# A two-layer diffusion block in float32: layer 0's gate and up products as Strassen's seven, its gated blocks through DRAM, and modulation pieces moved

## The chip, the cores and the metric

The kernel runs on one core of a Trainium2 chip. The metric is the device time of one execution in microseconds (us). The engines are TensorE (PE), VectorE (DVE), ScalarE (ACT), GpSimd (POOL) and SyncE (SP), which here only issues DMAs.

## The reference

Two layers over 512 latent and 256 context tokens of width 1024, all in float32. Each layer has modulated norms around an attention of three head groups, and around a gated feed-forward with hidden width 2816. What the change touches is the feed-forward and the modulation:

```python
def _swiglu(h, w_gate, w_up, w_down):
    return (jax.nn.silu(h @ w_gate) * (h @ w_up)) @ w_down
...
for l in range(DEPTH):
    last = l == DEPTH - 1
    mod = (silu_c @ w_ada[l] + b_ada[l])[:, None, :]
    mod_c = (silu_cc @ w_ada[l] + b_ada[l])[None, None, :]
    sh_a, sc_a, gt_a, sh_f, sc_f, gt_f = jnp.split(mod, 6, axis=-1)
...
    hf = _rms(x, g_ffn_pre[l]) * (1.0 + sc_f) + sh_f
    x = x + gt_f * _rms(_swiglu(hf, w_ffn_gate[l], w_ffn_up[l], w_ffn_down[l]), g_ffn_post[l])
    if not last:
        hfc = _rms(xc, g_ffn_pre[l]) * (1.0 + csc_f) + csh_f
        xc = xc + cgt_f * _rms(_swiglu(hfc, ...), g_ffn_post[l])
```

Layer 0 runs all 768 tokens through the feed-forward, layer 1 only the 512 latent ones.

## The kernel before, in words

**Precision.** A float32 product is made of three fast ones (`mm3`, L415): each operand is split into a rounded part and a residual (`copy`, L397, and `low`, L412, which computes x minus its rounded part). A weight tile is 128x1024 (four blocks of 128 rows by 256 columns, or two by 512): `weights` (L452) loads it (`st`), lets ACT write the rounded part `wh` and DVE or POOL the residual `wl`. Four of each are in a ring (`RING`).

**Order of the work.** Each stage collects steps in a `Plan` (L136), each with a rank, the engines that could do it with a cost for each, the steps it follows and the buffers it takes. `run` orders the steps by rank and by these costs and writes the program; the order on each engine is fixed from then on. The ranks come from a table of numbers at the head of the file.

**The stages**, the same in both layers: input projection (110 to 240 us in layer 0, 1137 to 1240 in layer 1), attention, out-projection (450 to 530; 1430 to 1475), gate and up (530 to 922; 1475 to 1713), down projection (922 to 1137; 1713 to the end). The out-projection takes the tokens in two passes; each token then gets its residual and norm (L703, L649), is modulated on DVE and POOL, transposed on PE (L663) and split into `hT`, the moving operand of gate and up. The chunk that follows runs in the same plan.

**Gate and up.** The hidden columns go in 11 chunks of 256. Chunk 0 (L1700) is plain in both layers. In layer 0 chunks 1 to 10 are plain too (L1890): per 128 hidden columns, 96 weight blocks are each multiplied with 512 latent and with 256 context tokens. ACT then takes silu of the gate, DVE multiplies it with up (L1899) into `a`, which stays in SBUF. In layer 1 chunks 1 to 10 (`by_sums`, L1749) are Strassen's product of a 2x2 split: the first two operands halve the tokens and the 1024 inputs, the other two are gate and up. Seven products of half size (L1813) take differences of weight tiles (`minus`, L1768, DVE or POOL) with sums of halves of `hT` (`sums_of_halves`, L1584), and their results are added up by DVE out of PSUM (L1841) and by DVE or POOL in SBUF (L1842, L1851 to L1862).

**Down.** `spread` (L1728) splits a block of `a` into the operand `sp`; `projected` multiplies it with the weights in two passes over the tokens of layer 0.

**Modulation.** `ada` (L486) makes one piece of 512 columns of `mod`: eight weight tiles of 256 KB are loaded, and DVE multiplies each with one scalar per partition and adds it to a sum (first L509, then seven times L511, a "mac"). A piece with two strands does so for `c` and for `c_ctx`; with one only for `c`. Each strand is split like an operand (L413) and summed over partitions by two matmuls of 512 columns (L527). Layer 0's gate and up holds 14 pieces with 20 strands; layer 0's input projection holds five pieces.

```python
for s, a in enumerate(acc):
    def mac(_, s=s, a=a, k=k, st=st):
        c = sc[:, s, k:k + 1]
        if k == 0:
            V.tensor_scalar(out=a.tile[:, :512], in0=st.tile[:, :512], scalar1=c, ...)
        else:
            V.scalar_tensor_tensor(out=a.tile[:, :512], in0=st.tile[:, :512], scalar=c,
                                   in1=a.tile[:, :512], op0=ALU.mult, op1=ALU.add)
```

## Time and profile before

| | us |
|---|---|
| median of 3 runs | 1841.51 (1840.59 to 1846.79) |
| the profiled execution | 1841.75 |
| its span in the trace | 1839.9 |
| PE busy | 1740.1 (95%) |
| DVE, ACT, POOL busy | 1245.7, 869.1, 880.3 |
| layer 0, gate and up from the first matmul to the last | 529.6 to 921.7 |
| layer 0, down projection | 922 to 1137 |
| layer 1, input projection | 1137 to 1240 |
| layer 1, gate and up | 1475.2 to 1713 |

The span is what the trace covers; the 1.85 us that the execution's own time has more lie around it. PE is busy nearly all the time, so its busy share alone says where it is slowed only where it falls; matmuls overlap in the records, and the time that one adds is the distance between two starts, not the length of a record. DVE and POOL records include time in which an operation stands still, so their means are compared with the same operation elsewhere.

### The profile page before, as it was taken

Reading aid. Unit: us, or ns where it says so; the run is one execution under the profiler, and the core shown is the slowest. Engines: PE = TensorE matmul, PEld = TensorE weight load, DVE = VectorE, ACT = ScalarE, POOL = GpSimd, SP = SyncE. Lnnn points to the kernel's source line nnn. Section 1 sums busy time; section 2 is a strip of 40 time slices with the busy share of each in tenths; the row PEclk is TensorE's granted clock in tenths of the full one; section 3 lists DMA queues with packets and bytes.
Section 4 is the critical chain, followed back from the end, with each engine's and each line's share of the span. In section 5 each row is a group of like instructions: output and inputs, shape, how many; then the busy total and the mean of one; then the engine's idle time right before and its main releaser. Section 6 shows DMA issues by size and latency. Waiting matters only on the chain. (4 is left out here: it accounts for less than half of the span.)

```text
span 1839.9 us, 28101 instructions
## 1 busy us (share of the span) xinstructions
PE 1740.1 (95%) x10290; PEld 1502.0 (82%) x10290; DVE 1245.7 (68%) x1728; ACT 869.1 (47%) x1792; POOL 880.3 (48%) x935
## 2 busy tenths in 40 slices
PE   6888799999999999999999898999999989999998
PEld 2676588788789888888888787978788789999886
DVE  6859878887575987521244745248989699998434
ACT  3344278997561221111233434538888545555212
POOL 3566967787362121000012628696878366543100
PEclk9889999999999999999999999999999999999999
DMA  9155103002644677321253432312101643331432
GB/s 309 58 151 161 51 22 84 13 2 71 212 142 123 209 223 252 124 71 46 82 182 126 137 126 91 93 53 53 44 2 62 202 161 116 126 103 59 160 95 77
DMA packets 135210, 205.79 MB, mean 112 GB/s; under 512 B 12920, under 2 KB 68696, under 8 KB 135072
## 3 DMA queue, kind: packets, MB, share of 16 engines
q1 hardware_dynamic: 135072, 203.99, 35.2%
q8 instruction: 81, 1.33, 0.3%
q14 instruction: 57, 0.47, 0.1%
HBM read 184.21 MB, written 9.52 MB: 105 GB/s over the span
## 5 line engine op out<-in xcount | busy, mean ns | idle before, releaser
L472 ACT CAST wh<-st 128x1024 fp32r<-128x1024 f32 (+2 forms) x177 | 183.5, 1039 | 337.5 <-PE m L419 141.4
L413 DVE TENSOR_TENSOR wl<-st,wh 128x1024 fp32r<-128x1024 f32 (+1 forms) x152 | 213.1, 1403 | 191.3 <-ACT wh L472 189.1
L1890 PE MATMUL m<-hT,wh 128*128 128x512 f32 (+1 forms) x1280 | 278.2, 339 | 0.0
L1890 PEld LDWEIGHTS m<-hT,wh 128*128 128x128 f32 x1280 | 196.6, 188 | 30.7 <-issue 0.8
L1385 ACT ACTIVATE P<-s,nm 128x768 f32<-128x768 f32 (+1 forms) x200 | 164.4, 826 | 25.8 <-DVE nm L1378 19.8
L417 PE MATMUL m<-wh,sp 128*128 128x512 f32 x440 | 171.9, 391 | 0.0
L418 PE MATMUL m<-wl,sp 128*128 128x512 f32 x440 | 171.5, 390 | 0.0
L419 PE MATMUL m<-wh,sp 128*128 128x512 f32 x440 | 171.3, 389 | 0.0
L1378 DVE TENSOR_REDUCE nm<-s 128x1 f32<-128x768 f32 x160 | 151.1, 950 | 23.5 <-PE s L1372 19.8
L1890 PE MATMUL m<-hT,wl 128*128 128x512 f32 (+1 forms) x640 | 164.7, 338 | 0.0
L511 DVE SCALAR_TENSOR_TENSOR acc<-st,sc,acc 128x512 f32<-128x512 f32 x182 | 141.8, 820 | 17.0 <-DMA st<-in_w_ada 15.9
L1813 PE MATMUL m<-hT,wh 128*128 128x256 f32 x800 | 145.0, 283 | 0.0
L418 PE MATMUL m<-wl,hT 128*128 128x512 f32 (+2 forms) x368 | 141.1, 383 | 3.0 <-DVE wl L413 1.8
L417 PE MATMUL m<-wh,hT 128*128 128x512 f32 (+2 forms) x368 | 143.3, 389 | 0.1
L419 PE MATMUL m<-wh,hT 128*128 128x512 f32 (+2 forms) x368 | 140.8, 383 | 2.6 <-POOL hT L413 2.6
L1813 PEld LDWEIGHTS m<-hT,wh 128*128 128x128 f32 x800 | 124.8, 192 | 0.0
L1813 PE MATMUL m<-hT,wl 128*128 128x256 f32 x400 | 113.4, 283 | 3.3 <-DVE wl L413 3.3
L1890 PEld LDWEIGHTS m<-hT,wl 128*128 128x128 f32 x640 | 98.7, 189 | 15.3
L413 DVE TENSOR_TENSOR wl<-x,wh 128x1024 fp32r<-128x1024 f32 x67 | 100.3, 1500 | 6.6 <-ACT wh L1773 6.5
L399 POOL TENSOR_SCALAR sp<-a 128x384 fp32r<-128x384 f32 (+1 forms) x11 | 9.0, 819 | 196.3 <-PE m L419 190.6
L1773 ACT CAST wh<-x 128x1024 fp32r<-128x1024 f32 x67 | 70.0, 1051 | 68.5 <-PE m L1813 33.5
L413 POOL TENSOR_TENSOR PT<-P,PT 128x384 fp32r<-128x384 f32 x93 | 95.6, 1033 | 3.7
(347 smaller groups left out, 4210.2 us busy)
## 6 DMA issues: line engine op xcount, KB each, us to landing
st<-in_w_ada SPq DMA_DIRECT2D x152, 256.0 KB
st<-in_w_ffn_down SPq DMA_DIRECT2D x66, 512.0 KB
...
```

The source lines that it names most:

```text
L399: G.tensor_scalar(out=out, in0=in_, scalar1=1.0, scalar2=0.0, op0=ALU.mult, op1=ALU.add)
L413: by(e).tensor_tensor(out=out, in0=src, in1=h.bitcast(F32), op=ALU.subtract)
L417: mm(ps, lhsT=a[0], rhs=b[0], start=start, stop=False)
L418: mm(ps, lhsT=a[0], rhs=b[1], start=False, stop=False)
L419: mm(ps, lhsT=a[1], rhs=b[0], start=False, stop=stop)
L472: a = plan.add(rank, {"act": c_act(W) + 0.05}, lambda _: A.copy(out=part(0)[:, :W], in_=st.tile[:, :W]), [x], kept[:1], [st])
L511: V.scalar_tensor_tensor(out=a.tile[:, :512], in0=st.tile[:, :512], scalar=c, in1=a.tile[:, :512], op0=ALU.mult, op1=ALU.add)
L1378: V.tensor_reduce(out=nm[:, 0:1], in_=S.tile[:, :768], axis=AX.X, op=ALU.max, negate=True)
L1385: A.activation(out=P.tile[:, c], in_=S.tile[:, c], func=AF.Exp, bias=box["nm"][:, i:i + 1], scale=1.0, accum_out=r_()[:, t + i:t + i + 1])
L1773: a = plan.add(rw, {"act": c_act(1024) + 0.05}, lambda _: A.copy(out=kept[0].tile, in_=x.tile), after, kept[:1], [x])
L1813: mm(m.tile[:, :n], lhsT=ww, rhs=moving[y](q, k), start=bool(first) and k == 0 and t == 0, stop=k == 3 and t == 2, skip_group_check=not first)
L1890: mm(o, lhsT=w, rhs=y[:, a:b, z, :], start=(k == 0 and i == 0), stop=(k == NK - 1 and i == 2))
```

## The change

Layer 0's gate and up become seven products in all 11 chunks. The tokens are put in the order of the two passes ([4, 5, 0] and [1, 2, 3]), which are the two halves of 384 tokens; so products have 384 columns, 168 of them a chunk. Layer 1's chunk 0 becomes seven products too, with 256 columns. Those products of chunks 0 to 2 which need only pass 1's tokens (1 and 2, 144 matmuls) are put ahead of the rest, beside pass 2's norms. In layer 0 the gated blocks are stored to DRAM by SP (`a_d`, 44 stores of 128x384) and read back in the down projection; and there the differences of weights and the sums and products in SBUF are POOL's alone (`only`, from chunk 1's second half on; chunks 0 and 1 begin on both). Of the 14 pieces of modulation in that stage four stay (6 strands); six go to layer 0's down projection (10 strands), four to layer 1's input projection (4 strands), where `P` has four buffers in place of seven.

```diff
-S_RANK = 26
+S_RANK = 5
-W_LATER = ((2, 512), (3, 0), (3, 512), (4, 0), (4, 512))
+W_LATER = (((2, 512), (3, 0), (3, 512), (4, 0), (4, 512)), ((3, 0), (3, 512), (4, 0), (4, 512)))
+F_LATER = ((0, 5, 0), (0, 5, 512), (1, 5, 0), (1, 5, 512))
+D_LATER = ((1, 0), (1, 512), (0, 0), (0, 512), (2, 0), (2, 512))
+D_ADA = (9, 12, 15, 18, 32, 38)
-F_ADA_STEP = 0.85
+F_ADA_STEP = 4.5
...
-            nw = W_PAIRS if l == 0 else 0
+            nw = W_PAIRS
...
+        if last:
+            aT = [fs.tile([128, TQ], F32, name=f"a{j}") for j in range(2)]
+        else:
+            a_d = [drp.tile([128, TQ], F32, name=f"ad{j}") for j in range(NH)]
...
+        parts7 = {1: ("a", "A11", 1), 5: ("c", "S1", 1), 7: ("d", "S3", 1), 6: ("b", "S2", 1), 2: ("a", "A12", 0),
+                  3: ("c", "S4", 0), 4: ("d", "A22", 0)}
...
+            def first(self, plan, rank, after=(), ways=("pool", "dve")):
+                l1, l2, self.l3 = (self.load(plan, rank, *q, after) for q in ((0, 0), (1, 0), (1, 1)))
+                x1, x2, x3 = self.xs[0, 0], self.xs[1, 0], self.xs[1, 1]
+                if self.whole:
+                    O[1] = self.split(plan, rank, x1, [l1])
+                t1 = self.minus(plan, rank, x1, x2, x1, [l1, l2, ...], ways)
+                O[5] = self.split(plan, rank, x1, [t1])
+                self.t3 = self.minus(plan, rank, x2, x3, x2, [self.l3, t1], ways)
+                O[7] = self.split(plan, rank, x2, [self.t3])
...
+                v = vec(both, plus(s7, s5, s7), [c.copied["c", jj], c.copied["d", jj]], (), [s5, s7])
+                u = vec({"dve": c_vec(n)}, psum_add(w, w, mb), [c.done[6, jj], c.copied["a", jj]], (), [w, mb])
+                y = vec({"dve": c_vec(n)}, psum_add(s5, w, mc), [c.done[3, jj], u, v], (), [w, s5, mc])
+                z = vec(both, plus(s7, w, s7), [u, v], (), [w, s7])
...
+                y = vec(both, lambda e, s5=s5, g1=g1: times(s5.tile, s5, g1)(e), [y, g], (), [s5, g1])
+                x = vec(both, lambda e, s7=s7, w=w: times(s7.tile, s7, w)(e), [z, x], (), [s7, w])
+                c.out += [(i, j, t, d) for i, (t, d) in enumerate(((s5, y), (s7, x)))]
+        def stored(plan, ch, rank):
+            for i, j, t, d in cs[ch].out:
+                plan.add(rank, {"sp": c_dma(n)}, lambda _, t=t, i=i, j=j: dma(
+                    out=a_d[j][:, i * n:(i + 1) * n], in_=t.tile), [d], (), [t], lag=2.2, writes=[("a", j, i)])
...
+            for ch in range(3):
+                columns_of(plan, ch, 20 + ch, 20 + ch, (1, 2), {i: w_f(plan, O_W0[l] + ch, ch, 0, u)
+                                                                for u, i in enumerate((1, 2))})
+            sums_of_halves(plan, full, S_RANK, taken)
+            ops[0].first(plan, O_W1[l], lds)
+            columns_of(plan, 0, 30, 30, (5, 7, 6, 3, 4), ops[0].second(plan, O_W1[l], lds))
+            ops[1].first(plan, O_W1[l] + 2, lds)
...
+                    after = [plan.add(rank - 1, {"sp": c_dma(w)}, lambda _: dma(out=rd.tile, in_=a_d[k][:, c0:c0 + w]), (),
+                                      [rd], lag=2.2, reads=[("a", k, pi)])]
...
+                for i, (al, v, c0) in enumerate(F_LATER):
+                    ada(plan, F_ADA[l] + F_ADA_STEP * i, al, v, c0, 2 - al, tiles, late=True)
+            only = ("pool", "dve") if last else ("pool",)
+            for ch in range(1, NH // 2):
+                if ch > 1:
+                    ops[ch].first(plan, rw, (), only)
+                columns_of(plan, ch, 2 * ch, 2 * ch + 1, (5, 7, 6, 3, 4) if ch <= 2 else (1, 5, 7, 6, 2, 3, 4),
+                           ops[ch].second(plan, rw, (), only), only)
+                if not last:
+                    stored(plan, ch, 2 * ch + 1)
...
+                for rk, (v, c0) in zip(D_ADA, D_LATER):
+                    ada(plan, rk, l + 1, v, c0, 2 if v < 2 else 1, tiles, late=True)
```

The change makes the lines of common functions three to five higher: `low` is L416, `copy` L402 or L404, the macs L512 and L514, the differences L1657, the products L1713, sums out of PSUM L1737, products and sums in SBUF L1740 and L1743, the stores L1767.

POOL, in a chunk of layer 0's gate and up past the first four, as the change orders it (`X`, `x` are weight tiles, `n` results of products): four differences and eight operations on results, which is a chunk's share.

```order
L1743 TENSOR_TENSOR n_4582<-n_4580,n_4582 128x384
L1743 TENSOR_TENSOR n_4590<-n_4588,n_4590 128x384
L1743 TENSOR_TENSOR n_4582<-n_4585,n_4582 128x384
L1743 TENSOR_TENSOR n_4590<-n_4589,n_4590 128x384
L1657 TENSOR_TENSOR X_4578<-X_4575,X_4578 128x1024
L1657 TENSOR_TENSOR X_4575<-x,X_4575 128x1024
L1657 TENSOR_TENSOR X_4578<-x,X_4578 128x1024
L1740 TENSOR_TENSOR n_4580<-n_4580,n_4583 128x384
L1740 TENSOR_TENSOR n_4588<-n_4588,n_4593 128x384
L1740 TENSOR_TENSOR n_4582<-n_4582,n_4585 128x384
L1740 TENSOR_TENSOR n_4590<-n_4590,n_4589 128x384
L1657 TENSOR_TENSOR x<-x,X_4578 128x1024
```

None of these stood there before: POOL had in layer 0's gate and up 25 instructions, for modulation pieces and the next stage.

DVE, in the third and fourth chunk of that stage, as the change orders it (`nf` are parts of a modulation piece, `m` is PSUM):

```order
L514 SCALAR_TENSOR_TENSOR nf<-nf,sc 128x512
L416 TENSOR_TENSOR wl<-X_4578,wh 128x1024
L1737 TENSOR_TENSOR n_4580<-n_4587,m_4600 128x384
L1737 TENSOR_TENSOR n_4582<-n_4588,m_4598 128x384
L514 SCALAR_TENSOR_TENSOR nf<-nf,sc 128x512 x2
L416 TENSOR_TENSOR wl<-X_4575,wh 128x1024
L1737 TENSOR_TENSOR n_4587<-n_4587,m_4599 128x384
L514 SCALAR_TENSOR_TENSOR nf<-nf,sc 128x512
L1737 TENSOR_TENSOR n_4588<-n_4588,m_4604 128x384
L514 SCALAR_TENSOR_TENSOR nf<-nf,sc 128x512
L416 TENSOR_TENSOR wl<-X_4578,wh 128x1024
L514 SCALAR_TENSOR_TENSOR nf<-nf,sc 128x512 x3
```

The residuals now come from tiles that POOL has made by subtraction, with macs between them; from the fifth chunk on the macs end.

DVE in the first pass of layer 0's down projection, before:

```order
L413 TENSOR_TENSOR wl<-st,wh 128x1024 x2
L413 TENSOR_TENSOR sp<-a_5640,sp 128x384
L413 TENSOR_TENSOR wl<-st,wh 128x1024 x2
L413 TENSOR_TENSOR sp<-a_5642,sp 128x384
L413 TENSOR_TENSOR wl<-st,wh 128x1024 x2
L413 TENSOR_TENSOR sp<-an,sp 128x384
```

and now:

```order
L416 TENSOR_TENSOR nr<-nf,nr 128x384
L416 TENSOR_TENSOR wl<-st,wh 128x1024
L514 SCALAR_TENSOR_TENSOR acc_8238<-st_8273,sc,acc_8238 128x512
L514 SCALAR_TENSOR_TENSOR acc_8241<-st_8273,sc,acc_8241 128x512
L416 TENSOR_TENSOR wl<-st,wh 128x1024
L514 SCALAR_TENSOR_TENSOR acc_8238<-st_8289,sc,acc_8238 128x512
L514 SCALAR_TENSOR_TENSOR acc_8241<-st_8289,sc,acc_8241 128x512
L514 SCALAR_TENSOR_TENSOR acc_8238<-st_8296,sc,acc_8238 128x512
L514 SCALAR_TENSOR_TENSOR acc_8241<-st_8296,sc,acc_8241 128x512
L514 SCALAR_TENSOR_TENSOR acc_8238<-st_8329,sc,acc_8238 128x512
L514 SCALAR_TENSOR_TENSOR acc_8241<-st_8329,sc,acc_8241 128x512
L416 TENSOR_TENSOR nr<-nf,nr 128x384 x2
```

The pieces' macs stand between the residuals of weights and of operands (`nr` is the operand, split from a block that was read back), and half of the residuals of weights went to POOL.

## Rows read from the trace of the kernel before

**Rows 1.** The page, part 1: busy time, share of the span, instructions

```profile
PE 1740.1 (95%) x10290; PEld 1502.0 (82%) x10290; DVE 1245.7 (68%) x1728; ACT 869.1 (47%) x1792; POOL 880.3 (48%) x935
```

**Rows 2.** Windows by stage: length, busy time (instructions) of each engine, clock, DMA

```profile
110.00:240.00 130.00, 107.40 (x480) 85.30 (x479) 106.20 (x170) 53.41 (x144) 102.23 (x104) 0.93 0.37 111
570.00:922.00 352.00, 348.64 (x1965) 298.75 (x1965) 196.74 (x272) 67.59 (x97) 34.86 (x25) 1.00 0.46 145
1137.00:1240.00 103.00, 100.54 (x503) 87.45 (x502) 34.20 (x65) 42.30 (x117) 86.38 (x116) 1.00 0.24 72
1504.00:1560.00 56.00, 51.06 (x406) 50.46 (x407) 52.69 (x55) 27.39 (x45) 32.03 (x22) 0.97 0.53 170
1560.00:1713.00 153.00, 153.00 (x1276) 152.96 (x1275) 138.96 (x148) 77.09 (x115) 70.83 (x63) 1.00 0.31 94
...
922.00:1020.00 98.00, 96.88 (x432) 79.76 (x431) 48.30 (x49) 38.83 (x59) 27.23 (x31) 1.00 0.46 149
```

**Rows 3.** PE's waits, 110 to 240 us, then 570 to 922: us, times, longest

```profile
PE m L527 <- ACT pair L401: 8.5, 2, 4.3
PE m L527 <- POOL pair L413: 5.5, 4, 2.5
...
PE m L527 <- DVE pair L413: 2.4, 2, 1.8
```

**Rows 4.** Line 1890 on PE: count, duration min/median/max, first and last start

```profile
L1890 PE MATMUL m<-hT,wh x1280: 277/337/500, 569.8 to 921.3; 128*128 128x512 f32 x92, 128*128 128x256 f32 x91
```

**Rows 5.** Timeline of PE: start, length, instruction; pairs of 512 and 256, then 384 columns

```profile
172.98 0.34 PE L418 MATMUL m<-wl,qaTh 128*128 128x384 f32 x1
173.15 0.34 PE L419 MATMUL m<-wh,qaTl 128*128 128x384 f32 x1
173.32 0.34 PE L417 MATMUL m<-wh,qaTh 128*128 128x384 f32 x1
...
700.81 0.51 PE L1890 MATMUL m<-hT,wl 128*128 128x512 f32 x2
...
701.85 0.51 PE L1890 MATMUL m<-hT,wl 128*128 128x512 f32 x2
```

**Rows 6.** DVE by line and form, 1137 to 1240, then macs, then 1504 to 1713

```profile
L413 DVE TENSOR_TENSOR wl<-st,wh 128x1024 fp32r<-128x1024 f32 x2 | 2.4, 1218 | 1.7 <-ACT wh L472 1.7
...
L511 DVE SCALAR_TENSOR_TENSOR P<-ast,sc,P x66: 729/740/2887, 116.7 to 205.0; 128x512 f32<-128x512 f32 x66
...
L1841 DVE TENSOR_TENSOR n<-n,m 128x256 f32<-128x256 f32 x40 | 16.1, 409 | 1.1 <-PE m L1813 1.1
```

**Rows 7.** POOL by line and form, 1137 to 1240, then whole span

```profile
L413 POOL TENSOR_TENSOR wl<-st,wh 128x1024 fp32r<-128x1024 f32 x6 | 14.3, 2397 | 8.0 <-ACT wh L472 8.0
...
L413 POOL TENSOR_TENSOR PT<-P,PT 128x384 fp32r<-128x384 f32 x93 | 95.6, 1033 | 3.7
```

**Rows 8.** Timeline of DVE, then of POOL, in layer 1's products

```profile
1613.78 1.70 DVE L413 TENSOR_TENSOR wl<-x,wh 128x1024 fp32r<-128x1024 f32 x1
...
1613.67 0.73 POOL L1855 TENSOR_TENSOR an<-an,n 128x256 f32<-128x256 f32 x1 [1.89 <-ACT n L1861]
1614.36 3.40 POOL L1862 TENSOR_TENSOR an<-an,n 128x256 f32<-128x256 f32 x2
```

**Rows 9.** DVE, then POOL, by line and form, 1504 to 1560

```profile
L413 DVE TENSOR_TENSOR wl<-x,wh 128x1024 fp32r<-128x1024 f32 x16 | 23.5, 1477 | 0.0
L413 DVE TENSOR_TENSOR sp<-a,sp 128x512 fp32r<-128x512 f32 x1 | 0.7, 678 | 0.0
...
L1768 POOL TENSOR_TENSOR x<-x 128x1024 f32<-128x1024 f32 x2 | 6.0, 2986 | 3.6 <-DVE wl L413 3.6
L1842 POOL TENSOR_TENSOR n<-n 128x256 f32<-128x256 f32 x4 | 5.8, 1468 | 5.2 <-ACT n L401 3.7 <-DVE n L401 1.5
```

**Rows 10.** Timeline of PE at layer 0's first gate matmul and last transposes

```profile
529.60 3.27 PE L1700 MATMUL m<-hT,yT 128*128 128x256 f32 x26
543.89 0.60 PE L663 MATMUL m<-ident,sb 128*128 128x128 f32 x4
```

443 lines of the change are left out of this document (205 added, 238 removed).

## The prediction

> **What bounds the kernel now.** The page's first part comes first: PE is busy 95% of the span [rows 1]. The windows by stage then show where that is not so: PE fills layer 0's gate and up (348.6 of 352 us) and the second part of layer 1's (153.0 of 153), and has holes in layer 0's input projection (107.4 of 130) and at the start of layer 1's products (51.1 of 56) [rows 2]. PE's waits name who ends the holes: in the first input projection it waits for the rounded and the residual part of modulation pairs, 8.5 and 5.5 us, and in layer 0's gate and up for 2.4 us in all [rows 3]. So fewer matmuls are worth their time, as long as VectorE and GpSimd (DVE, POOL) can feed them; both are near idle in layer 0's gate and up as it stands for POOL (34.9 of 352), while DVE has 196.7 [rows 2].
>
> **What is removed.** In layer 0, 10 chunks of 96 pairs of matmuls (512 and 256 columns) stand between 569.8 and 921.3 us [rows 4]. Three pairs take 1.04 us in mid-stream [rows 5], 0.347 each, and a matmul of 256 columns 0.120 (1276 in 153.0 us, [rows 2]), so one of 512 takes 0.227. Less the 40 row sums L527 of 20 strands at that price (9.1) and 2.4 us of waits for pairs [rows 3], 340 us are left for 960 pairs, 0.354 each. Chunk 0 has 288 matmuls of 256 columns, 34.6 us. The seven products need 11 chunks x 168 = 1848 matmuls of 384 columns. Matmuls of 384 columns start every 0.174 us where they occur now [rows 5], so 322 us instead of 374: **-52 us of PE** in layer 0. Layer 1's chunk 0 falls from 192 to 168 of 256 columns: -2.9 us. Of the row sums 28 leave the stage; 20 go to layer 0's down projection (4.5 us) and 8 to layer 1's input projection (1.8 us), so they cancel over the run.
>
> **What is added: work for DVE and POOL.** A chunk of layer 0 now needs four differences of weights (128x1024) and eight sums and products (128x384) on POOL, and seven residuals (128x1024) on DVE. Alone, a 1024-wide operation costs DVE 1.22 us and POOL 2.40, a 384-wide one 1.03 on POOL, a mac L511 0.74 [rows 6, 7]. What decides is that the two engines hinder each other. In layer 1's products the DVE residual that starts at 1613.78 takes 1.70 us, with a POOL operation from 1614.36; POOL's two 256-wide ones there take 3.40 us, where one at 1613.67 took 0.73 [rows 8]. Means from 1504 to 1560 tell the same: 1.48 for 1.22 on DVE, 1.47 for 0.73 on POOL [rows 9], yet DVE operations that read PSUM keep to 0.41 [rows 6]. So DVE operations with two SBUF inputs and POOL operations share something, and their undisturbed times have to be added. How much of the sum fits into a microsecond is read where PE has holes and both have work, 1504 to 1560: DVE 27 operations of 1024, eight of 512 and three of 256, 32.9 + 5.4 + 1.2 = 39.5 us; POOL two of 1024, 15 of 256, three residuals and two casts of 512, 4.8 + 11.0 + 3.8 + 1.3 = 20.9 [rows 6 to 9] (rows 9 show the largest groups; the others repeat these forms). That is 60.4 in 56 us, **1.08 per us**. From 1560 to 1713, at about 0.93 by the same count, PE has no hole [rows 2].
>
> The Trainium skill (SBUF — State Buffer, section "SBUF: two separate sides") says that the pair of ports that DVE and GpSimd share is an exclusive lock, held for a whole instruction, and that a DVE operation with two SBUF inputs takes it against a GpSimd operation that reads SBUF. The rows agree but for the 8% that fits in beside. By the rule taken strictly the sum would come out as the second rival below; it speaks against this change, which gives POOL long work next to DVE's.
>
> **Layer 0's gate and up under this sum.** The steady chunk needs 4 x 2.40 + 8 x 1.03 + 7 x 1.22 = 26.4 us, 24.4 at 1.08, against 168 x 0.174 = 29.2 of PE: hidden. The first chunks also carry pass 2's norms, the sums of halves, 6 of the 20 strands of modulation, and this counts out otherwise. From pass 2's last transposes, 14.3 us after the first gate matmul [rows 10], until the operands of chunk 4 begin to stand, the order has on DVE 30 operations of 1024 (36.6 us), 41 macs (30.3) and 17 two-input operations of 512 at 0.68 [rows 9] (11.6); on POOL 16 of 1024 (38.4), 31 of 384 (31.9) and 15 of 512 at some 1.25, half of 2.40 and a little (18.8). Together 168 us, of which the last two products aren't waited for: 166, at 1.08 **154 us**. PE has in that stretch 624 matmuls, 109 us. So PE is late by 45 us at chunk 4, and from there 1176 matmuls, 205 us, follow without a hole. The stage ends 14.3 + 154 + 205 = 373 us after its first matmul, where it now ends 392 after (529.6 to some 921.6): **-19 us** instead of the -52 that PE's count gives. Bounds: at 1.04 it is -13; with PE some operands ahead of that stretch (four of each half are in the ring, 4.2 us each) -27.
>
> **Layer 0's down projection.** It takes six pieces, 10 strands; its first pass now has 98 us with DVE busy 48 and POOL 27 [rows 2]. In the order of the change that pass has on DVE 10 residuals, 59 macs, 8 residuals of 384 and 4 of 512, 63 us; on POOL 11 of 1024, 13 of 384, ten smaller, 49 us. 112 us at 1.08 are 104, against 396 x 0.227 + 3.6 = 93.5 of PE. Four weight tiles and four operands are ready when the pass starts, which covers most of the ten; I take 3 of 0 to 10, and 4.5 for the row sums: **+8**. The reads back of the blocks (44 of 196 KB) lie ahead of their use by the order and a DMA share of 0.46 there [rows 2] leaves room; nothing for them, up to 4 if the ring of three holds them up.
>
> **Layer 1's input projection.** Four strands, 28 macs and four first terms, 23 us, join 34 of DVE and 86 of POOL in 103 us [rows 2]. Without the small operations on both, about 117 us of two-input work stand in 103, 108 at 1.08. Taken: 2 of 0 to 5, and 1.8 for the row sums: **+4**. Four pieces' worth of holes, as in the first input projection (14 us for five pieces of two strands, [rows 3]), is the upper end, +10.
>
> **Layer 1's gate and up.** -2.9 of PE; against it 12 us more of DVE and POOL work in the early part, which is at the limit today. Between -3 and +8; the nearest row, PE's 5 us of holes there [rows 2], says that half of it shows: **0**.
>
> **The sum**: -19 + 8 + 4 + 0 = -7. The profiled execution took 1841.75 us, 0.24 over the median of 1841.51: 1834.8, so **1835 us**. A difference under 0.3%, 5.5 us, can't be told from none: below 1836.0 is faster, above 1847.0 slower.
>
> **Rivals.** *PE stays the bound* (chance 0.22): macs and differences wait for nobody, and DVE or POOL do what PE needs in the others' shadow. Then the stage ends at 14.3 + 1800 x 0.174 + 2.7 = 330 us, or 336 with the new waits of pass 2's transposes: -56; with 4.5 + 1.8 for row sums, -2.9 in layer 1 and some 4 of waits, -48: 1794 us. For it speaks that each engine alone has less than PE (98 and 89 us of 109 in the first chunks); against it the stretched rows.
>
> *Each operation waits the other out* (0.23), slower: nothing fits in beside, as where the two run back to back without a pause. It decides from about 1.03 per us on. At 1.0 the first chunks take 166 (-7), the down projection's first pass 112 (+18 less 8 of what stands ready, and the row sums: +15), the input projection 117 (+10) and layer 1 +4: +22; with a third of this lost again in pauses that the planner's order leaves, 1847 to 1868, as its point 1857 us. The 56 us at 1.08 are against it, the holes of the first input projection, with five pieces in it, for it. By the rule of the Trainium skill quoted above (SBUF — State Buffer) this would be the case to expect.
>
> *The queue of stores* (0.08): SP issues 44 stores, each waiting for POOL's last product of a half, with weight loads behind it. If a store stands 2 us a chunk ahead of a load that is wanted, 20 us of PE go: 1843 to 1855, or about no change, 1846. The order issues loads two chunks ahead, so I hold it unlikely.
>
> **How the numbers follow.** My forecast has 0.47. Its own range is 1822 (-27 in gate and up, +5, +2, 0) to 1850. Of it 0.26 lies below 1836.0, 0.13 within 5.5 us and 0.08 above. Faster: 0.22 + 0.26 = 0.48. Same: 0.13 and 0.05 of the queue's 0.08: 0.18. Slower: 0.23 + 0.08 + 0.03 = 0.34. The range for 8 in 10 takes in the nearer half of the first rival and most of the second: 1794 to 1858.
>
> **What would show it.** Right: gate and up of layer 0 in some 373 us, PE with holes in its first four chunks, ended by residuals on DVE or differences on POOL, and none in the last seven; the 1024-wide means at 1.5 on DVE and over 3 on POOL early, matmuls of 384 columns every 0.174 us. Wrong: no holes in the first chunks (first rival), holes in all eleven or in both passes of the down projection (second), or a wait for DMA at a weight (third).

## The result, and the profile after

| | before | after |
|---|---|---|
| median | 1841.05 us (1839.36 to 1846.79, 4 runs) | 1905.96 us (1902.08 to 1908.97, 4 runs) |
| ratio, 95% interval | | 1.0346 [1.0312, 1.0379] |
| profiled execution, span | 1841.75, 1839.9 | 1903.09, 1901.3 |

The change makes the kernel slower by 3.5%, outside the forecast's range. The page of the kernel after answers to [rows 1]: PE has 384 matmuls and 19 us of busy time less, DVE 177 us and POOL 274 us more; the mean granted clock of the profiled execution is 0.96, for 0.98 before.

```profile
PE 1720.8 (91%) x9906; PEld 1510.8 (79%) x9906; DVE 1423.1 (75%) x1816; ACT 943.5 (50%) x1906; POOL 1153.8 (61%) x1068
```

Where the time went is read from windows by stage, cut in both traces at the last projection matmul of each stage (columns as in [rows 2]: length, PE, PEld, DVE, ACT, POOL, clock, DMA share, GB/s). Before: layer 0's gate and up, its down projection, layer 1's input projection, attention, gate and up.

```profile
529.40:921.80 392.40, 387.02 (x2278) 336.10 (x2277) 221.18 (x300) 88.05 (x136) 61.86 (x48) 1.00 0.45 143
921.80:1112.40 190.60, 185.28 (x825) 152.71 (x824) 101.30 (x97) 75.41 (x116) 67.23 (x68) 0.99 0.43 139
1112.40:1236.80 124.40, 120.14 (x617) 104.31 (x617) 46.92 (x70) 53.49 (x138) 102.54 (x127) 1.00 0.27 81
1236.80:1425.80 189.00, 177.48 (x1274) 156.27 (x1273) 168.22 (x279) 158.30 (x367) 148.38 (x190) 0.98 0.14 39
...
1475.00:1712.60 237.60, 230.04 (x1890) 228.36 (x1889) 217.84 (x231) 119.44 (x184) 124.05 (x100) 0.99 0.36 113
```

After, the same five stages, and then layer 0's gate and up in two parts, the down projection's first pass, the same pass before, and 44 us of it after:

```profile
528.00:916.40 388.40, 341.05 (x1888) 334.45 (x1886) 289.64 (x269) 139.72 (x206) 263.54 (x159) 0.94 0.37 117
916.40:1140.50 224.10, 200.86 (x846) 157.09 (x846) 168.49 (x176) 85.96 (x139) 109.07 (x81) 0.95 0.67 217
1140.50:1274.00 133.50, 126.44 (x627) 107.85 (x625) 72.69 (x109) 58.67 (x148) 110.43 (x127) 0.97 0.44 139
1274.00:1473.80 199.80, 182.09 (x1275) 160.03 (x1273) 173.95 (x275) 159.20 (x366) 151.84 (x193) 0.95 0.13 33
...
1522.90:1773.70 250.80, 232.66 (x1867) 229.62 (x1867) 227.95 (x237) 124.34 (x196) 138.15 (x105) 0.97 0.35 108
...
528.00:720.00 192.00, 144.65 (x756) 138.63 (x755) 165.16 (x156) 69.08 (x113) 138.29 (x80) 0.88 0.45 141
720.00:916.00 196.00, 196.00 (x1131) 195.42 (x1130) 124.48 (x114) 70.33 (x93) 125.26 (x80) 1.00 0.30 94
...
916.40:1037.00 120.60, 104.46 (x414) 79.95 (x414) 97.26 (x95) 39.55 (x59) 58.68 (x37) 0.92 0.75 245
921.80:1011.80 90.00, 90.00 (x400) 74.53 (x399) 42.30 (x39) 31.39 (x42) 19.95 (x23) 1.00 0.47 152
976.00:1020.00 44.00, 36.84 (x144) 26.91 (x143) 43.53 (x41) 14.06 (x19) 25.27 (x13) 0.92 0.73 237
```

The differences are -4.0, +33.5, +9.1, +10.8 and +13.2 us; the other stages give -1.2 together, and the sum is the 61.4 us by which the spans differ. Length less PE's busy time says how much of each is holes. In layer 0's gate and up PE is busy 46.0 us less, as the products promise, and idle 42.0 us more (47.4 for 5.4). In the down projection it is idle 17.9 us more, and 15.6 us more busy, of which the 20 row sums that came there explain 4.5; nearly all of it, 30.6 us, is the first pass (120.6 us for 90.0), and the second takes 103.5 for 100.6. In layer 1's gate and up it is idle 10.6 us more, and busy 2.6 us more though it has 24 matmuls less: this goes with the clock, 0.97 for 0.99. All holes of layer 0's gate and up lie before 720 us: there the clock is 0.88, and from 720 on PE is busy 196.0 of 196.

Who ends the holes: PE's waits of the kernel after from 528 to 712 us, from 916 to 1141, from 1523 to 1774 and from 1274 to 1480 (us, times, longest).

```profile
PE m L1713 <- ACT n L404: 11.6, 2, 8.9
PE m L530 <- DVE nr L404: 10.4, 1, 10.4
PE m L530 <- POOL nr L402: 8.1, 1, 8.1
PE m L1713 <- DVE wl L416: 6.7, 4, 3.6
...
PE m L530 <- ACT pair L404: 7.7, 3, 3.5
PE m L530 <- DVE pair L416: 4.1, 3, 3.4
PE m L421 <- POOL wl L416: 4.0, 2, 2.1
...
PE m L1713 <- DVE wl L416: 10.4, 8, 2.6
...
PE s L1381 <- DVE Vg L416: 7.0, 1, 7.0
```

PE waits for parts of modulation pairs (`pair`, and `nr`, which holds them in this stage), for residuals of weights, and for copies out of PSUM. In none of these waits is a DMA what PE itself waits for, but behind one of them stands a load. The hole of 8.9 us ends at 597.85 with a copy by ACT that waited for a sum of POOL. Before that, from 580.4 to 586.4, DVE had stood idle for a weight tile whose load SP issued at 582.71, when a residual of POOL had just read its buffer (to 582.69). Neither the pieces' macs nor the stores make this hole: in the runs below without most macs and without stores (e1, e4) the same wait for ACT takes 9.5 and 9.2 us.

DVE and POOL from 528 to 720 us, by line and form, show the operations that are late; their prices alone are in [rows 6, 7].

```profile
L514 DVE SCALAR_TENSOR_TENSOR nf<-nf,sc 128x512 f32<-128x512 f32 x42 | 54.6, 1327 | 1.8 <-DMA nf<-in_w_ada 1.6
L416 DVE TENSOR_TENSOR wl<-X,wh 128x1024 fp32r<-128x1024 f32 x16 | 23.3, 1458 | 1.9 <-ACT wh L1663 1.9
...
L1657 POOL TENSOR_TENSOR X<-x,X 128x1024 f32<-128x1024 f32 x8 | 22.5, 2813 | 4.9 <-DVE wl L416 4.3 <-DMA x<-in_w_ffn_up 0.5
```

A mac takes 1.33 us in place of 0.74, a residual 1.46 in place of 1.22, a difference on POOL 2.81 in place of 2.40. The timeline of DVE, then of POOL, from 614 us shows how:

```profile
615.09 3.42 DVE L416 TENSOR_TENSOR wl<-x,wh 128x1024 fp32r<-128x1024 f32 x1
618.42 1.21 DVE L416 TENSOR_TENSOR wl<-X,wh 128x1024 fp32r<-128x1024 f32 x1
619.56 7.77 DVE L514 SCALAR_TENSOR_TENSOR nf<-nf,sc 128x512 f32<-128x512 f32 x4
...
614.69 2.73 POOL L1657 TENSOR_TENSOR X<-x,X 128x1024 f32<-128x1024 f32 x1
619.72 2.84 POOL L1657 TENSOR_TENSOR X<-x,X 128x1024 f32<-128x1024 f32 x1 [2.29 <-DVE wl L416]
```

The residual that begins at 615.09 ends at 618.51, 1.09 us after POOL's operation (614.69 + 2.73 = 617.42): it has stood through it. The next one, with POOL waiting for it, takes 1.21. The four macs from 619.56 take 7.77 us for 3, beside three operations of POOL.

What a hole can cost beyond itself stands in PE's timeline after the one of 3.59 us that ends at 558.57:

```profile
558.57 0.69 PE L1713 MATMUL m<-hT,wl 128*128 128x384 f32 x1 [3.59 <-DVE wl L416]
559.05 0.84 PE L1713 MATMUL m<-hT,wh 128*128 128x384 f32 x2
...
560.01 0.84 PE L1713 MATMUL m<-hT,wh 128*128 128x384 f32 x2
...
565.30 0.51 PE L1713 MATMUL m<-hT,wh 128*128 128x384 f32 x2
...
565.82 0.51 PE L1713 MATMUL m<-hT,wh 128*128 128x384 f32 x2
```

Three matmuls of 384 columns take 0.96 us after the hole and 0.52 six microseconds later, 0.32 and 0.174 each, a ratio of 1.84, which fits the two levels of the clock, 1.2 and 2.4 GHz, within 8%. After the two holes before it, of 2.64 and 2.67 us (ended at 541.79 and 552.26), the matmuls went on at some 0.175.

### The profile page after: what moved, and what is told of

It is laid out like the page before. It is cut to its first block, busy times and chain, and to the rows that moved or that the text cites. A ratio compares the mean times of both kernels' runs of the same rounds, so it can differ in the third digit from the quotient of the medians.

```text
span 1901.3 us, 28055 instructions
## 1 busy us (share of the span) xinstructions
PE 1720.8 (91%) x9906; PEld 1510.8 (79%) x9906; DVE 1423.1 (75%) x1816; ACT 943.5 (50%) x1906; POOL 1153.8 (61%) x1068
## 4 chain that ended last, share of the span: by engine, by line
PE 51%; DVE 19%; issue 9%; POOL 9%; DMA 5%; ACT 5%; SPq 1%; DVEq 0%; POOLq 0%; ACTq 0%
PE m L1713 20%; PE m L421 6%; PE m L422 6%; PE m L420 6%; PE s L1381 4%; DVE wl L416 3%; DVE acc L514 2%; PE m L1355 2%; DVE nf L514 2%; PE m L1498 2%; PE m L1439 2%; ACT P L1394 1%; DMA st<-in_w_ada 1%; DVE P L514 1%; PE m L1344 1%
## 5 line engine op out<-in xcount | busy, mean ns | idle before, releaser
L1713 PE MATMUL m<-Y,wh 128*128 128x384 f32 (+1 forms) x1408 | 312.8, 313 | 3.5 <-DVE Y L416 3.5
L1713 PE MATMUL m<-hT,wh 128*128 128x384 f32 (+1 forms) x1056 | 237.6, 316 | 13.8 <-ACT n L404 13.4
L1713 PEld LDWEIGHTS m<-Y,wh 128*128 128x128 f32 x1408 | 242.3, 194 | 4.0 <-DVE Y L416 3.7
L416 DVE TENSOR_TENSOR wl<-st,wh 128x1024 fp32r<-128x1024 f32 (+1 forms) x111 | 152.4, 1377 | 119.8 <-ACT wh L475 119.2
L1713 PE MATMUL m<-Y,wl 128*128 128x384 f32 (+1 forms) x704 | 221.3, 314 | 7.9 <-DVE wl L416 7.7
L1713 PEld LDWEIGHTS m<-hT,wh 128*128 128x128 f32 x1056 | 183.3, 195 | 16.0 <-ACT n L404 14.5
L1394 ACT ACTIVATE P<-s,nm 128x768 f32<-128x768 f32 (+1 forms) x200 | 164.6, 826 | 33.5 <-DVE nm L1387 11.8
L1713 PE MATMUL m<-hT,wl 128*128 128x384 f32 (+1 forms) x528 | 167.1, 317 | 9.3 <-DVE wl L416 9.3
L416 DVE TENSOR_TENSOR wl<-X,wh 128x1024 fp32r<-128x1024 f32 x80 | 140.0, 1750 | 33.8 <-ACT wh L1663 33.5
L1713 PEld LDWEIGHTS m<-Y,wl 128*128 128x128 f32 x704 | 136.4, 194 | 10.5 <-DVE wl L416 10.4
L1743 POOL TENSOR_TENSOR n<-n,n 128x384 f32<-128x384 f32 (+1 forms) x83 | 95.1, 1155 | 78.5 <-ACT n L404 34.1
L514 DVE SCALAR_TENSOR_TENSOR acc<-st,sc,acc 128x512 f32<-128x512 f32 x112 | 112.0, 1052 | 7.6 <-DMA st<-in_w_ada 7.4
L416 POOL TENSOR_TENSOR wl<-st,wh 128x1024 fp32r<-128x1024 f32 (+2 forms) x35 | 86.7, 2482 | 50.1 <-ACT wh L475 41.8
L421 PE MATMUL m<-wl,nr 128*128 128x512 f32 x264 | 106.4, 403 | 5.9 <-POOL wl L416 4.0
L1713 PEld LDWEIGHTS m<-hT,wl 128*128 128x128 f32 x528 | 103.0, 195 | 10.3 <-DVE wl L416 10.3
L638 POOL TENSOR_TENSOR r<-v,mhalf 128x1 f32<-128x1 f32 x42 | 30.6, 730 | 127.2 <-DVE v L723 102.3
```

What stands on the lines that cost most here:

```text
L416: by(e).tensor_tensor(out=out, in0=src, in1=h.bitcast(F32), op=ALU.subtract)
L421: mm(ps, lhsT=a[0], rhs=b[1], start=False, stop=False)
L1394: A.activation(out=P.tile[:, c], in_=S.tile[:, c], func=AF.Exp, bias=box["nm"][:, i:i + 1], scale=1.0, accum_out=r_()[:, t + i:t + i + 1])
L1713: mm(m.tile[:, :n], lhsT=ww, rhs=moving[y](z, k), start=bool(first) and k == 0 and t == 0, stop=k == 3 and t == 2, skip_group_check=not first)
L1743: return lambda e: by(e).tensor_tensor(out=out.tile, in0=x.tile, in1=y.tile, op=ALU.add)
```

## The experiments

Theory A: the moved pieces and POOL's operations hold each other up on the two engines, and PE, which takes its work in a fixed order, waits for pairs and residuals. Rival B: stores and loads in SP's queue, or their traffic, make operands late. Later a split of A was tested: A1, the row sums merely stand too early in PE's order; A2, DVE and POOL are full. Edits are against the kernel after, unless said. Each run named e is a single execution with its profile, so a total is compared with the four of the kernel after (1902.08 to 1908.97) only where it lies well outside them. Single stages repeat better: where an edit leaves one alone, layer 0's gate and up takes 388.2 to 389.6 us (after, e4, e7, e9, e10) and its down projection 222.9 to 224.1 (after, e3, e7).

**e1: nearly no macs.** The 14 pieces take one weight tile of eight; seven eighths of their macs and loads are left out, in gate and up, the down projection and layer 1's input projection.

```diff
-                    ada(plan, rk, l + 1, v, c0, 2 if v < 2 else 1, tiles, late=True)
+                    ada(plan, rk, l + 1, v, c0, 2 if v < 2 else 1, tiles, late=True, nk=1)
...
-        for k in range(NK):
+        for k in range(nk):
```

> The changed kernel, but each of the 14 modulation pieces in layer 0's gate and up, layer 0's down projection and layer 1's input projection multiplies only the first of its eight weight tiles (7 of 8 macs and loads are left out; row sums and all else stay). Theory A (DVE and POOL exclude one another, and the macs overload them; PE then waits at the row sums): the down projection falls from 224 to about 195 us, layer 1's input projection from 133 to about 125, layer 0's gate and up from 388 to about 350 with no wait of PE over 4 us; in all 1906 to about 1825. Theory B (the store queue on SP holds the loads): gate and up stays above 375, in all about 1865. Theory C (Strassen's own differences and sums on POOL are too many even without macs): gate and up stays near 380 and the down projection falls, in all about 1860.

Measured: 1843.59 us, 59.5 less than the profiled execution of the kernel after. The windows of gate and up and of the down projection of layer 0:

```profile
527.20:888.10 360.90, 336.06 (x1887) 330.77 (x1887) 248.45 (x233) 140.19 (x206) 247.44 (x153) 0.96 0.34 106
888.10:1090.60 202.50, 194.63 (x847) 156.36 (x846) 105.24 (x115) 79.09 (x128) 84.32 (x83) 0.97 0.58 186
```

Gate and up falls by 27.5 us, the down projection by 21.6, layer 1's input projection by 5.6 and its attention by 2.6. So the pieces' macs or loads make most of the loss, as A says; but even with them nearly gone the kernel is no faster than before, and A's 350 us for gate and up, its 1825 in all and its "no wait of PE over 4 us" were missed: PE still has 24.8 us of holes there, the longest of 9.5, so a part is theory C's, the new stage's own differences and sums. Beside before, 12 us stay in the down projection, 8 in attention and 12 in layer 1's gate and up. Macs and loads are taken apart below for the down projection; in gate and up they were not.

**e9 and e10: macs without loads, loads without macs.** e1 takes both away. Here the six pieces of layer 0's down projection keep one of the two. In e9 only the first tile of a piece is loaded, and all eight steps multiply it; in e10 all eight are loaded, and only the first is multiplied.

```diff
-            st = st_()
+            if k < loads:
+                st = st_()
-            x = plan.add(rk, {"sp": c_dma(512)}, lambda _, k=k, st=st: dma(
+            x = x if k >= loads else plan.add(rk, {"sp": c_dma(512)}, lambda _, k=k, st=st: dma(
...
+            if k >= macs:
+                continue
```

> The six pieces of layer 0's down projection load only their first weight tile of 256 KB and all eight steps of a strand multiply that one tile: 42 loads are left out, so their values are not the reference's; the 80 operations of DVE stay. Down projection of layer 0: 224.1 us in the changed kernel, 202.4 with seven of eight macs and loads gone, 190.7 before. If what costs is the time of DVE and POOL (macs beside residuals), it stays at 216 to 224. If it is SP's queue, where weight loads stand behind loads of pieces that wait for a mac to free their buffer (42.6 us in 26 waits of L500 for acc), or the traffic (a DMA share of 0.75 in the first pass), it falls to 200 to 208.

> The six pieces of layer 0's down projection load all eight weight tiles, but only the first is multiplied (70 of 80 operations of DVE left out, so their values are not the reference's). The loads now wait for no mac. Down projection of layer 0, 224.1 us in the changed kernel: if macs cost, as time of DVE and POOL or because loads wait for them, it falls to 200 to 206, as with macs and loads both gone (202.4). If the traffic costs, it stays over 210.

Measured: 1909.03 and 1897.31 us. The down projection in e9, and under it PE's longest wait there:

```profile
916.90:1145.40 228.50, 200.38 (x846) 158.40 (x845) 168.09 (x179) 82.20 (x134) 106.68 (x83) 0.94 0.51 164
...
PE m L533 <- DVE pair L416: 12.3, 5, 6.1
```

and in e10:

```profile
922.70:1133.60 210.90, 194.64 (x846) 155.15 (x845) 104.39 (x112) 81.34 (x132) 89.13 (x82) 0.98 0.70 230
```

Without loads, so that no load of a piece stands in SP's queue waiting for a mac, and with the DMA share down from 0.67 to 0.51, the stage is no shorter: 228.5 us for 224.1, with 28.1 us of holes for 23.2 at nearly the same clock. (A mac that waits for no load comes sooner, so the macs may stand in thicker clumps; this was not separated.) Without macs it falls by 13.2 us, to 210.9. That is 8.4 us more than in e1 with neither, and just over the bound of 210 that the text had put for the traffic, so the loads have some price too when the macs are gone; but e1 also thins the pieces in gate and up ahead, and the comparison is not clean. What the two runs show is that the loads by themselves do not make the loss, and that the macs, that is the time of DVE and POOL, make 13.2 of its 33.5 us. Of the 12 us that stay in e1, 4.5 are the row sums, 2.6 are holes, and the rest goes with a clock of 0.97 for 0.99.

**e3: either engine.** Layer 0's differences, sums and products may go to POOL or DVE, as in layer 1.

```diff
-            only = ("pool", "dve") if last else ("pool",)
+            only = ("pool", "dve")
```

> The changed kernel, but in layer 0 the differences of weights and the sums and products may go to DVE or POOL, as in layer 1. Theory A (the two engines share one way to SBUF): a 1024-wide difference holds it 1.22 us on DVE and 2.40 on POOL, so moving some to DVE makes the sum smaller, but in layer 0's first chunks the macs stay: 5 to 15 us less, 1890 to 1900. A rival (POOL alone is the bottleneck there): 25 us or more less. Another rival (DVE is the bottleneck, which is why POOL was made the only one): slower than 1906 by 10 us or more.

Measured: 1887.53 us; layer 0's gate and up takes 370.3 us in place of 388.4, the other stages are within 3.2 us. In all it is 15.6 us less than the profiled execution of the kernel after, a little more than the 5 to 15 of theory A and well short of the rival's 25.

```profile
529.50:899.80 370.30, 340.01 (x1888) 334.57 (x1887) 303.40 (x345) 140.93 (x210) 131.90 (x80) 0.95 0.39 123
```

POOL is relieved of 131.6 us, DVE takes up 13.8. The same work is a heavier load on POOL, for itself and for those operations of DVE that have two inputs in SBUF, which stand for as long. That "POOL alone" costs some 16 us by itself was not in the forecast.

**e4: no stores.** The 44 stores are left out, and the down projection reads other data of the same size, so its values are not the reference's.

```diff
-            if not last:
-                stored(plan, 0, 0)
...
-                if not last:
-                    stored(plan, ch, 2 * ch + 1)
```

> The changed kernel without the 44 stores of gated blocks to DRAM (the down projection reads a part of the stored residual stream in their place, as many bytes). Theory B (stores wait for POOL at the head of SP's queue and hold the weight loads behind them): layer 0's gate and up falls by 15 us or more. Theory A (DVE and POOL): it stays within 6 us of 388, since PE's long waits there are at the row sums of pieces and at results of products, and 1906 falls by less than 8.

Measured: 1899.84 us; gate and up 388.3 (388.4 with stores), down projection 218.8 (224.1). The queue waits 123.1 us in 38 stores for POOL's products (L1767) in the kernel after, and the stage takes the same time without them: as the cause of the loss there the stores fall. The down projection's 5.3 us lie outside what that stage varies by. Where the 5.3 us of the down projection come from was not looked into.

**e5: the two engines by themselves.** A kernel of its own, which computes nothing of the reference: 30 subtractions of 128x1024 on DVE alone, then DVE beside POOL (of the 16 meant for POOL alone only the first ran alone, 2.34 us; the others met DVE's next ones), then DVE with one input in PSUM beside 15 on POOL, then macs of 512 beside 30 of 384 on POOL.

```python
dve(30, a, b)
gps(15, c, e)
...
for _ in range(60):
    V.tensor_tensor(out=d[:, :512], in0=a[:, :512], in1=m, op=ALU.subtract)
gps(15, c, e)
```

> The disputed price by itself, and nothing of the reference: subtractions of 128x1024 tiles in SBUF, 30 on DVE alone, 16 on POOL alone, then 30 on DVE beside 15 on POOL; then 60 DVE subtractions of 128x512 that read one operand from PSUM beside 15 on POOL; then 40 macs of 512 on DVE beside 30 subtractions of 384 on POOL. Theory A (they exclude one another): alone 1.2 us and 2.4 us each; together the 45 take 1.0 to 1.1 times less than 36.5 + 36 = 72.5, that is 66 to 73 us; the 60 with PSUM and the 15 take no longer than the longer of the two, about 42 us; the macs and the 384-wide ones take 57 to 61 us. If they only slow one another by sharing a bandwidth, the pairs take 45 to 55 us and both slow alike.

Measured, in timelines of the second stretch and the fourth, and for the third by line and form:

```profile
101.30 3.24 DVE L30 TENSOR_TENSOR d<-a,b 128x1024 f32<-128x1024 f32 x1
103.54 3.20 POOL L34 TENSOR_TENSOR p<-c,e 128x1024 f32<-128x1024 f32 x1
104.58 3.24 DVE L30 TENSOR_TENSOR d<-a,b 128x1024 f32<-128x1024 f32 x1
...
198.32 1.32 POOL L34 TENSOR_TENSOR p<-c,e 128x384 f32<-128x384 f32 x1
198.82 1.36 DVE L51 SCALAR_TENSOR_TENSOR d<-a,col,d 128x512 f32<-128x512 f32 x1
...
L46 DVE TENSOR_TENSOR d<-a,m 128x512 f32<-128x512 f32 x52 | 35.8, 688 | 1.8
L34 POOL TENSOR_TENSOR p<-c,e 128x1024 f32<-128x1024 f32 x15 | 35.3, 2352 | 1.2
```

They take strict turns. A DVE operation and one of POOL take 3.28 us together (101.30 to 104.58), where alone they have records of 1.23 and 2.34: 1.09 us of records per us, as theory A had it (1.0 to 1.1). POOL's operation ends at 106.74, DVE's next at 107.82, so each stands until the other has ended, and only about 0.15 us of its own record goes on beside. A mac and a 384-wide one take 1.40 us (198.32 to the next at 199.71), for 0.75 and 1.01 alone; all 40 and 30 took 52.0 us, less than A's 57 to 61. With one input in PSUM nothing is lengthened: all 60 records of DVE have 0.686 to 0.689 us, with POOL working or not, and POOL's 2.35.

**e7: layer 1's first chunk plain.** Chunk 0 of layer 1 as before, layer 0 as after (the diff's core):

```diff
-                                      whole=(0, 1) if pi == 0 else (1,))
+                                      whole=(0, 1) if pi == 0 or last else (1,))
...
+            if last:
+                plain(plan, 0, 20, 20, [[w_f(plan, O_W0[l] + 2 * gu + u, 0, gu, u) for u in range(2)] for gu in range(2)])
+                sums_of_halves(plan, full, 24, taken)
```

> The changed kernel, but layer 1's chunk 0 is plain and stands whole between the last norms and the first seven products, as before the change; layer 0 is as changed. Theory A: layer 1's gate and up (251 us) loses the early differences and sums of chunk 0 and goes back to 237 to 242, and nothing else moves: 1906 to about 1895. The rival (that stage is slow because of what precedes it, the input projection and attention of layer 1 ending later and at a lower clock): it stays at 248 or more.

Measured: 1889.73 us; the stage takes 238.1 us for 250.8, and 237.6 before, and nothing else moves by more than 2.5. Its window, where PE has 24 matmuls more and yet 1.1 us less of busy time:

```profile
1522.20:1760.30 238.10, 231.57 (x1891) 229.53 (x1890) 216.52 (x231) 120.27 (x190) 119.98 (x97) 0.99 0.33 102
```

The +13 of layer 1's gate and up is wholly its own first chunk, which brought differences and sums to the stretch where [rows 9] had found the engines at their limit.

**e8: row sums later.** In PE's order the row sums go 60 to 110 matmuls later in gate and up and 12 to 30 in the down projection.

```diff
-            end = [plan.add(rank, {"pe": 2 * c_mm(512) if rows else 0.95}, add_up, [x, y, *(end if s else [])],
+            end = [plan.add(rank + (2.0 if late else 0), {"pe": 2 * c_mm(512) if rows else 0.95}, add_up, [x, y, *(end if s else [])],
```

> The changed kernel with the row sums of the pieces in layer 0's gate and up and down projection put later on PE: in gate and up some 60 to 110 matmuls (10 to 20 us), in the down projection 12 to 30 matmuls (3 to 7 us). Theory A1 (PE stands at a row sum because the pair is late, and everything behind it in PE's queue waits with it, though its operands are there): the 23 us at row sums and the columns' transpose in gate and up fall under 8, those 12 in the down projection under 6; 1906 to about 1885. Theory A2 (the products behind the row sum would have waited for DVE anyway, since DVE and POOL are full): the waits only change their name, to residuals and sums, and the time stays within 8 us of 1906.

Measured: 1899.15 us; gate and up 384.9, down projection 223.2. PE's waits in the one and in the other:

```profile
PE m L1713 <- ACT n L404: 12.1, 2, 9.4
PE m L1713 <- DVE n L1737: 8.1, 1, 8.1
PE m L530 <- DVE nr L404: 7.4, 1, 7.4
...
PE m L421 <- DVE wl L416: 7.8, 7, 2.8
```

The holes change their names and stay: in gate and up 42.5 us for 47.4, with 12.9 at row sums where A1 said under 8; in the down projection 26.7 for 23.2, with 9.6 where it said under 6. A2 holds: what PE waits for is mostly whatever DVE and POOL have not come to, and A1 falls.

**n1 and n2: the pieces back, and a part of layer 0 plain.** Chunks 0 to 4 of layer 0 (n2: 0 to 6) are plain, in two halves of 384 columns; the rest are seven products on either engine; all 14 pieces are back in gate and up; layer 1's chunk 0 is plain; the blocks still go through DRAM.

```diff
+NPLAIN = (5, 1)
-F_ADA_STEP = 4.5
+F_ADA_STEP = 1.0
...
+                if ch < NPLAIN[l]:
+                    plain(plan, ch, 2 * ch, 2 * ch, W[1] if ch == 1 else
+                          [[w_f(plan, rw, ch, gu, u) for u in range(2)] for gu in range(2)])
```

> Seven products only where DVE and POOL have room: in layer 0 chunks 0 to 4 are plain (four tile residuals each, nothing on POOL), chunks 5 to 10 are the seven products on either engine; all 14 modulation pieces are back in layer 0's gate and up, none in the down projection and none more in layer 1's input projection; layer 1's chunk 0 is plain. Theory A (what DVE and POOL do with two SBUF inputs adds up, and the pieces' macs overloaded them): gate and up needs 345 us of PE for products, 9 for row sums, and 340 of DVE and POOL, so 360 to 372 us against 392 before; down projection 190 to 196; layer 1's input projection and attention as before (124 and 189); layer 1's gate and up 236 to 242; in all 1812 to 1828. The rival (the loss sits in the read back from DRAM and in how the new stage is laid out, not in the pieces): down projection stays over 210, in all over 1845.

> As n1_mixed with chunks 0 to 6 plain and four chunks of seven products. Theory A: 9.5 us more of PE than n1_mixed, but 40 less for DVE and POOL: if those still bind in n1_mixed, this is as fast or faster (1812 to 1825); if PE binds there, it is 8 to 10 us slower.

Measured: 1839.89 us, ratio to before 0.9999 [0.9983, 1.0014], and 1837.79, 0.9986 [0.9969, 1.0003]. Both intervals take in 1. In n1 the down projection takes 191.9 us, the input projection 124.7, attention 188.4 and layer 1's gate and up 238.2, all within 1.3 of before: what the change lost behind layer 0's gate and up came with the pieces and layer 1's first chunk, and the way through DRAM costs about 1 us at most there. But gate and up of layer 0 takes 389.0 (n2: 386.5), not the 360 to 372 that I had expected, and the total misses 1812 to 1828 with it. The window of n1 from 600 to 700 us shows DVE full with macs while POOL has time:

```profile
600.00:700.00 100.00, 91.70 (x502) 83.81 (x501) 92.97 (x128) 26.17 (x39) 21.51 (x13) 1.00 0.70 212
```

**n3 to n6: spreading the pieces.** n3 is n1 with the pieces 1.25 of a rank step apart in place of 1.0, two buffers for pairs, and 2.5 us reckoned from a pair's residual to its row sum; n4 the same with three plain chunks and a step of 1.3. In n3 one long hole stayed:

```profile
785.66 1.01 PE L1714 MATMUL m<-Y,wh 128*128 128x384 f32 x2 [10.62 <-DVE nf L405]
```

A product waits 10.6 us for a bank of PSUM that a copy of a row sum holds, and this copy stands behind macs and residuals in DVE's queue. In n4 the longest is 5.5 us, for another bank, which DVE's product of gate and up (L1798) frees. n5 gives the copy to ACT; n6 does so with four plain chunks and a step of 1.3.

```diff
-NPLAIN = (5, 1)
+NPLAIN = (4, 1)
-F_ADA_STEP = 1.25
+F_ADA_STEP = 1.3
...
-            x = plan.add(rank, {"act": c_act(512), "dve": c_vec(512)}, lambda e: copy(e, row.tile[:2, :512], ps.tile[:2, :]),
+            x = plan.add(rank, {"act": c_act(512)}, lambda e: copy(e, row.tile[:2, :512], ps.tile[:2, :]),
```

> n1_mixed (five plain chunks, six of seven products) with the pieces spread over the whole stage (a step of 1.25 in place of 1.0), two buffers for pairs in place of one and the row sums 2.5 us later for the planner. In n1_mixed DVE was busy 93 of 100 us from 600 to 700 and 75 of 90 at the end, and PE lost some 17 us at row sums. Theory A: with DVE's load even over the stage PE loses under 12 us in all: gate and up 366 to 376 us, in all 1815 to 1828. If the loss stays at 25 us or more, the macs bind wherever they stand, and it is as before, about 1838.

> As n3_mixed5 with three plain chunks and eight of seven products, step 1.3: 9.5 us less of PE and some 35 more for DVE and POOL. Theory A: those bind, and it is slower than n3_mixed5 by 5 us or more. The rival (only the first chunks matter): up to 9 us faster than n3_mixed5.

> n3_mixed5 with the copy of a row sum out of PSUM on ACT alone. In n3_mixed5 PE lost 10.6 us in one piece: a product waited for the PSUM bank that such a copy on DVE frees, and the copy stood behind macs and residuals in DVE's queue. Theory A: that wait goes and nothing takes its place: gate and up 376 to 380 us, in all 1823 to 1828. The rival (DVE is late there in any case, and PE only waits for its next residual): 1832 or more.

> The same with four plain chunks and seven of seven products, step 1.3: 4.7 us less of PE, some 18 more for DVE and POOL. Theory A: within 4 us of n5_act5, since what PE gains DVE loses; clearly slower (6 us) if DVE binds, clearly faster if there was room.

| | median us | ratio to before | layer 0, gate and up, us |
|---|---|---|---|
| n3 | 1835.41 | 0.9975 [0.9961, 0.9989] | 388.9 |
| n4 | 1837.74 | 0.9986 [0.9974, 0.9997] | 385.8 |
| n5 | 1832.34 | 0.9963 [0.9950, 0.9975] | 380.8 |
| n6 | 1827.08 | 0.9933 [0.9919, 0.9946] | 379.2 |

The stage is that of one profiled execution. For n3 this is the slowest of its ten (1842.76), for n4 the fastest (1830.75), so this column does not rank them. The forecasts fared badly: n3's 366 to 376 us for the stage was missed; n4 against n3 was neither 5 us slower nor faster, and their intervals overlap; n5 came out at the rival's 1832 or more. Its intervals and n3's overlap too, and the wait has not gone, it is shorter:

```profile
PE m L1714 <- ACT nf L405: 6.1, 1, 6.1
```

n6, with one chunk more of seven products, is 5.3 us faster than n5, and their ranges do not meet (1825.30 to 1828.15, and 1830.37 to 1833.76); but in their profiles only 1.6 us of 6.0 lie in this stage, and why the rest, where the two programs do the same work, is faster in n6 was not found.

n6 is faster than the kernel before by 12 us, or 0.7%, whose median beside it was 1838.99. Its down projection takes 191.1 us; its window of layer 0's gate and up:

```profile
529.80:909.00 379.20, 361.33 (x2015) 348.67 (x2014) 337.14 (x423) 131.29 (x203) 109.03 (x73) 0.98 0.53 169
```

PE saves 25.7 us of busy time (387.0 before) and gives 12.5 back in holes, with DVE's records filling 337 of 379 us, in part with standing still.

## Why the prediction was wrong

**What bounds the kernel, and the price of the products** were right. PE is busy 341.1 us for 387.0 in layer 0's gate and up, and matmuls of 384 columns start every 0.174 us at the full clock. The forecast of 52 us less in matmuls becomes 46 us of busy time, at a clock of 0.94.

**The shared time of DVE and POOL** was right in kind and in its rate. e5 finds 1.09 us of records per us where both have work without end; the forecast had 1.08. This is partly luck, since the 1.08 was read from one window of 56 us with macs nowhere in it, and e5 has 1.26 for short operations. It finds also that each operation stops the other, so forecast and second rival were no two mechanisms: the 8% "that fits in beside" is the start of each record. The Trainium skill (SBUF — State Buffer, section "SBUF: two separate sides") calls this an exclusive lock held for a whole instruction; e5's strict turns agree, at 1.08 us for DVE and 2.20 for POOL of a 1024-wide pair's 3.28, but for the 0.15 us of each record. By the strict rule I had put 1.0 per us, and e5 has 1.09.

**Layer 0's gate and up: -19 forecast, -4 measured.** The shape was as said: holes in the first chunks and none in the last seven. What ended them was only in part what the text had named: residuals 6.7 us, but pairs of the pieces 19.5 and copies out of PSUM 11.6; and POOL's differences took 2.81, not over 3. The step that failed is "at 1.08": it took for the whole early stretch a rate that holds where neither engine ever pauses. The work itself was counted well. Counted as in the forecast, at undisturbed durations, the operations that began between 542.3 and 711.8 us (where the last seven chunks begin) come to 167 to 173 us (an estimate; the shortest records of each form, or those a tenth of the way up, are taken as its duration alone); the forecast had 168. They took 169.5 us, about 1.0 per us, in place of 154, and these 15.5 us are the whole miss. From 528 to 720 us DVE stood idle 26.8 of 192 us, 7.6 of it before sums that wait for POOL's results and 9.9 for loads.

PE's side of the same stretch reads otherwise. It was idle 43.5 us there, and the forecast had made it late by 45; but it was busy 126.1 us, at a granted clock of 0.88, where the forecast had 109 for its products at full speed (654 matmuls ran there, with row sums and transposes, for the 624 it counted). Whether PE would have been done sooner at the full clock, or would only have waited longer for DVE and POOL, no run separates. The second rival's term for this stage, -7, came nearer, with its reason half wrong: not its rate but the pauses it mentioned in passing.

**Layer 0's down projection: +8 forecast, +33.5 measured.** This is the term that was furthest off. Two steps failed. One is "four weight tiles and four operands are ready when the pass starts, which covers most of the ten": PE is busy for the first 20 us, but the pass took 120.6 us, and not even the 104 without any cover. The other is again "112 us at 1.08 are 104": the same count over the pass's trace gives 112 us of work, so the count was right and the rate was 0.93 per us. In the trace the work comes in clumps: from 976 to 1020 us DVE is busy 43.5 of 44 while PE, at its place in a fixed order, stands idle 7.2 us for a pair or a residual that stands behind macs; between 916 and 936 DVE had been busy for 6.1 of 20. e9 and e10 show that macs make 13.2 us of the loss and that the loads alone do not make it; e8 shows that moving the sums does not help. The holes grow by 17.9 us and the busy time by 15.6, where 4.5 was forecast for the row sums.

**The clock was not in the sum at all.** Beside gate and up, 11 us of the down projection's busy time go with a granted clock of 0.95 for 0.99. In the input projection 4.5 us of busy time beyond its 8 row sums go with 0.97 for 1.00, in attention 4.6 with 0.95 for 0.98, and in layer 1's gate and up 2.6 and the 2.9 that its fewer matmuls should have saved with 0.97 for 0.99: some 26 us in the four stages behind layer 0's gate and up. This is an estimate from the windows, not an experiment of its own. A hole costs itself and, as the timeline above shows for one of 3.59 us, it can cost matmuls at the lower clock behind it.

**Layer 1's input projection: +4 forecast, +9.1 measured**, within the bounds (+10). **Attention: +10.8.** The sum had nothing for it, without a reason. Its first scores wait 7.0 us for `Vg`, where they waited 2.5. With the macs nearly gone (e1) the stage still takes 8 us more than before, and in n1, with the pieces out of the stage ahead and `P` with its seven buffers, it is back at 188.4; whether the buffers alone do this was not tried. **Layer 1's gate and up: 0 forecast, +13.2 measured**, beyond the bound of +8; e7 shows that it is its own first chunk. "Half of it shows" was the failed step: the holes grew by 10.6 us, nearly the whole of the 12 us of added work, and the 2.9 us less of matmuls were given back at the lower clock.

**The rivals.** PE as the bound without holes (1794) is refuted by 47.4 us of holes. The queue of stores is refuted by e4 for gate and up. The second rival had the right side and the right mechanism, and was short by 49 us, for the same three reasons: clumps, the clock, and layer 1. Its point does not follow from its own terms: +22 alone is 1864, and pauses would add to that, where the text has 1857. A smaller slip is the 2.4 us of waits for pairs "in all", which is the row of DVE's pairs alone; with ACT's and POOL's it is 3.4, which changes nothing. Against the 1835 forecast, 68.4 us of the spans' difference came from elsewhere: 15 in gate and up, 25.5 in the down projection, 5.1, 10.8 and 13.2 in layer 1, and -1.2 in the rest.
